# Per-token factors by a DRAM round trip instead of transposes, with a table of put-off steps, in a two-layer hybrid attention encoder

## The chip, the cores and the metric

The kernel runs on one core of a Trainium2 chip. A core has a matrix engine (TensorE, PE in the profile), VectorE (DVE), ScalarE (ACT), GpSimd (POOL) and SyncE (SP). SP computes nothing here: it issues DMAs. All engines run their own instructions in order and wait for each other by semaphores. The metric is the device time of one execution in microseconds.

## The reference, cut to what matters

512 tokens of width 1024 pass through two layers. In each layer a mixer A (8 query heads, 2 key heads, window 128, with a sink logit) and a mixer B (three head groups with other windows and dilations) run on one joint projection of x. What the change touches is how the attention outputs are scaled, token by token:

```python
# mixer A, per block:   e = exp(s - m);  denom = sum(e) + exp(sink - m)
o = einsum('nkgqs,nskd->nqkgd', e, vj) / denom
# mixer B: three group outputs, weighted per position and head slot
wts = softmax(stack(lses), axis=0)
ob = einsum('gbsh,gbshd->bshd', wts, stack(outs))
```

Then both outputs go through a branch projection, are gated (`ga * ya + gb * yb`), projected out, normalised, and followed by an MLP, a gated per-layer embedding and a second normalisation.

## The kernel before

All products are made in three passes of a float32r split: each matrix is cut into a high and a low part (`split`: ACT casts to the high part, DVE subtracts to get the low one), and hi*hi, lo*hi and hi*lo are summed (`mm3`). Weights come as tiles of 128x1024 by SP (`wst`, three buffers), are cut, and then used; some (`LATER`) are cut by `split_later`, where ACT writes -hi and an accumulating DMA issued by POOL adds the weights to it (tile `wlo`). A fetch by SP waits until the buffer's earlier weights are cut.

The attention block of a layer is one loop over small steps, `attention_block`. TensorE's order is fixed by hand while it is recorded: generators yield conditions on a forecast clock `fc`, and in each round the loop takes the first step that is due out of `side` (small helper units) and `live` (at most two attention units), and otherwise a step of the filler, which is three 128x512 matmuls of a projection (names `ps_(...)`), a gate or, at the end, the branch-A product `ya`. The other engines' order is settled by a scheduler that sees the whole program.

There are four A units (`unit_a`, names `a0` to `a3`, each two heads), six B units (`unit_b`, names `b`, pair 0 or 1, group 0 to 2) and two mixings (`mix_b`). A unit's steps on TensorE are scores (`sa`, `sb`), transposes of the probabilities (`pta`, `ptb`), and value products (`oa`, `ob`). Between them DVE masks the scores, ACT takes exponentials, ACT and DVE cut the transposed probabilities (`pth`, `ptl`). The result f (`fa`, `ogb`) has head dimensions on its 128 partitions and the 512 tokens along its rows.

The factors (`den` for A, `e` for B) come out the other way: a token is a partition. To multiply f by them, `widened` lets ACT write the factor 64 times into a 128x512 tile `wide`, four TensorE transposes turn it (tiles `rsa`, `rs`, in PSUM), and DVE multiplies (`token_scaled`). A layer does that four times for A and six times for B, 40 transposes in all. Then `split` makes the operands OA and OB of the branch products.

When the block is over, the residual tiles `y`, the embedding input `pf` and rows of constants are loaded by SP, `pf` is cut (`ph` by ACT, `pl` by DVE), and the branch products run: gates `g`, `ya` for A (which needs OA), then `yb` for B (which needs OB). A gate's projection is read out of its PSUM bank by a tanh on ACT (tile `gate`); there are three such banks (tag `mm`), taken in turn by projections, gates and `ya`.

Of the kernel before, what the change touches and what calls it, by code (L numbers as in the profile page):

```python
# [10 lines left out]
F32 = mybir.dt.float32  # L11
# [3 lines left out]
ALU = mybir.AluOpType  # L15
# [5 lines left out]
P = 128  # L21
S = 512
# [14 lines left out]
        ("b", 1, 0), ("b", 1, 1), ("b", 1, 2), ("g", 4), ("g", 5), ("y", 0), ("y", 1), ("g", 6), ("g", 7), ("y", 2), ("y", 3)]  # L37
PASSES = ((0, 0), (0, 1), (1, 0))
HOP = 0.35
ACTIVE = 2  # L40

QB0, KB0, VB0, GL0 = 768, 1536, 2304, 3072

# [158 lines left out]
def build(nc, tc, plan, down, xT, xN, pT, wst, vec, rows, sink, cst, out):  # L202
# [3 lines left out]
    with ctx:  # L206
# [142 lines left out]
        def attention_block(l, av, rp, vt, OA, OB, begun):  # L349
# [101 lines left out]
                fc.give("o", t)  # L451
                return t

            def widened(c, name, after):
                wide = av.tile([P, 4, 2, 64], F32, tag="wide", name="wide" + name, bufs=1)
                nc.scalar.copy(wide, c.rearrange("p r (j u) -> p j r u", u=1).to_broadcast([P, 4, 2, 64]))
                return wide, fc.on("act", 0.52, after) + HOP

            def token_scaled(f, wide, name, after):
                R = bank("pt", "rs" + name)  # L460
                for j in range(4):
                    nc.tensor.transpose(R[:, j * P:(j + 1) * P], wide[:, j].rearrange("p r d -> p (r d)"), ident)
                nc.vector.tensor_tensor(f, f, R, ALU.mult)
                t = fc.on("dve", 0.6, max(fc.pe(0.43) + HOP, after)) + HOP
                fc.take("pt", t)
                return t


            WIN = [(max(0, P * (j - 1)), min(S, P * (j + 2))) for j in range(4)]
# [2 lines left out]
            def unit_a(i):  # L472
# [26 lines left out]
                nc.scalar.activation(se, se, AF.Exp)  # L499
                nc.vector.tensor_tensor(den, den, se, ALU.add)  # L500
                nc.vector.reciprocal(den, den)
                wide, t_wide = widened(den, nm_, ex[1, 3] + 0.6)
                yield lambda: "va" in held
                v, t_v = held["va"]
                f = av.tile([P, S], F32, tag="f", name="f" + nm_, bufs=1)
                groups = [(r, kbs) for r in range(2) for kbs in ((0, 3), (1,), (2,))]
                done = []

# [35 lines left out]
                held["P"] -= 2  # L544
                if i == 3:
                    held["vv"] -= 1
                yield lambda: fc.open("pt") and fc.t >= t_wide
                t_f = token_scaled(f, wide, nm_, t_f)
                split(OA[i][0], OA[i][1], f)
                forecast_split(S, t_f)  # L550


            WIN0 = [(max(0, P * j - 64), min(S, P * j + 192)) for j in range(4)]
# [111 lines left out]
            def mix_b(sp, cn, cs):  # L665
# [33 lines left out]
                for g in range(3):  # L699
                    nc.vector.tensor_tensor(e[:, g], e[:, g], mn, ALU.mult)  # L700
                t += 2.6
                for g in range(3):
                    f, t_f, _ = fs[g]
                    wide, t = widened(e[:, g].rearrange("p (s b) -> p s b", s=2), f"{nm_}_{g}", t)
                    yield lambda: fc.t >= t and fc.open("pt")
                    token_scaled(f, wide, f"{nm_}_{g}", t_f)
                    t = fc.t
                f = fs[0][0]
                nc.gpsimd.tensor_tensor(f, f, fs[1][0], ALU.add)
                nc.vector.tensor_tensor(f, f, fs[2][0], ALU.add)  # L710
                split(OB[sp][0], OB[sp][1], f)

            sk = av.tile([P, 8], F32, tag="sk", name=f"sk{l}", bufs=1)
            nc.scalar.dma_start(sk, sink[l])
# [37 lines left out]
            def filler():  # L752
                def project(key, sigma_order):
                    yield lambda: held["qk"] - held["free_qk"] < 5
                    held["qk"] += 1
                    ps = yield from steps((l, key), X)
                    held[key] = rope(ps, sigma_order, "_".join(str(v) for v in (l, *key)))

                for kind, *idx in FLOW:
                    if kind == "qa":  # L760
                        yield from project(("qa", *idx), False)
                    elif kind == "b":
                        yield from project(("qb", *idx), idx[1] > 0)
                        yield from project(("kb", *idx), idx[1] > 0)
                        ps = yield from steps((l, ("vb", *idx)), X)
                        nm_ = "vb" + "_".join(str(v) for v in (l, *idx))
                        v, t = values(ps, "sigma" if idx[1] else "edge", nm_)
                        side.append([v_unit(("vb", *idx), v, t, nm_), None])
                    elif kind == "g":
                        ps = yield from steps((l, ("g", 0, *idx)), X)  # L770
                        ga.append(gate(l, 0, idx[0], vt, rp, ps))
                        fc.give("mm", fc.on("act", 0.57, fc.t + HOP) + HOP)
                    else:
                        yield lambda: not any(k[0] == "a" for k in (*waiting, *live))
                        u = idx[0]
                        w = weights((l, ("ba", u)))
                        fc.on("dve", 1.135, fc.on("act", 0.947, fc.t + HOP) + HOP)
                        for n, g in enumerate(ga[2 * u:2 * u + 2]):
                            yield lambda: fc.open("mm")
                            ps = bank("mm", f"ya{l}_{u}_{n}")  # L780
# [13 lines left out]
                    return True  # L794
                return ok

            ga, waiting, live = [], {}, {}
            for i in range(4):
                waiting["a", i] = (slots(2, "ka", ("qa", i)), lambda i=i: unit_a(i))
            for sp in range(2):  # L800
# [5 lines left out]
                waiting["m", sp] = (lambda sp=sp: not any(k[:2] == ("b", sp) for k in live),  # L806
                                    lambda sp=sp, cn=cn, cs=cs: mix_b(sp, cn, cs))
            with tc.manual_schedule(engines={PE}):
                side.append([v_unit("va", va, t_va, f"va{l}"), None])
                fill, fill_ok, idle = filler(), None, 0  # L810
                while waiting or live or side or fill:
                    if waiting and len(live) < ACTIVE:
                        key = next(iter(waiting))
                        ok, make = waiting[key]
                        if ok():
                            del waiting[key]
                            live[key] = [make(), None]
                    moved = False
                    for key, g in [(None, g) for g in side] + list(live.items()):
                        if g[1] is None or g[1]():  # L820
                            try:
                                g[1] = next(g[0])
                            except StopIteration:
                                if key is None:
                                    side.remove(g)
# [17 lines left out]

        def gate(l, b, t, vt, rp, ps=None):
            ps = linear((l, ("g", b, t)), X) if ps is None else ps
            g = rp.tile([P, S], F32, tag="gate", name=f"gate{l}_{b}_{t}", bufs=11)
            nc.scalar.activation(g, ps, AF.Tanh, bias=vt["half"][:, b * 8 + t:b * 8 + t + 1], scale=0.5)
            return g

# [209 lines left out]
        for l in range(DEPTH):  # L1059
# [31 lines left out]

            M = []
            for u in range(4):
                gs = [gate(l, 1, t, vt, rp) for t in (2 * u, 2 * u + 1)]
                w = weights((l, ("bb", u)))
                for n, g in enumerate(gs):
                    t = 2 * u + n
# [268 lines left out]
```

## Time and profile before

| | us |
|---|---|
| median of three runs | 1539.62 |
| the three runs | 1536.09, 1539.66, 1539.62 |
| the profiled execution's own time | 1536.4 |
| its span in the trace | 1534.6 |
| TensorE busy | 1512.5 (99% of the span) |
| DVE, ACT, POOL busy | 1017.7, 763.7, 246.4 |

The span runs from the first to the last instruction; 1.8 us of the time lie around it. TensorE's matmuls are pipelined and their ends are modelled, so that a busy TensorE can still hold gaps: the starts of neighbouring matmuls tell more than their durations. The two attention blocks lie at about 29 to 264 and 792 to 1032 us.

### The profile page before, as it was taken

Reading aid. Unit: us, or ns where it says so; the run is one execution under the profiler, and the core shown is the slowest. Engines: PE = TensorE matmul, PEld = TensorE weight load, DVE = VectorE, ACT = ScalarE, POOL = GpSimd, SP = SyncE. Lnnn points to the kernel's source line nnn. Section 1 sums busy time; section 2 is a strip of 40 time slices with the busy share of each in tenths; the row PEclk is TensorE's granted clock in tenths of the full one; section 3 lists DMA queues with packets and bytes.
Section 4 is the critical chain, followed back from the end, with each engine's and each line's share of the span. In section 5 each row is a group of like instructions: output and inputs, shape, how many; then the busy total and the mean of one; then the engine's idle time right before and its main releaser. Section 6 shows DMA issues by size and latency. Waiting matters only on the chain.

```text
span 1534.6 us, 19685 instructions
## 1 busy us (share of the span) xinstructions
PE 1512.5 (99%) x7438; PEld 1243.0 (81%) x7438; DVE 1017.7 (66%) x1751; ACT 763.7 (50%) x1244; POOL 246.4 (16%) x213
## 2 busy tenths in 40 slices
PE   9999999999999999999999999999999999999996
PEld 7778888888888888888887888878888888888885
DVE  5666553558568777686876665534585776767868
ACT  5777764344344443444557776633442444444442
POOL 1212220110011120202012112111100201111022
PEclk9999999999999999999999999999999999999998
DMA  7544665345612414141355445574455233231403
GB/s 234 124 112 111 149 151 166 123 137 152 205 55 87 133 54 153 42 161 59 100 168 137 114 112 138 138 209 134 149 149 183 69 109 111 82 124 56 151 1 96
DMA packets 53951, 189.47 MB, mean 123 GB/s; under 512 B 6496, under 2 KB 6880, under 8 KB 53856
## 3 DMA queue, kind: packets, MB, share of 16 engines
q1 hardware_dynamic: 43200, 151.74, 30.0%
q0 software_dynamic: 9936, 36.18, 12.5%
q8 instruction: 58, 0.95, 0.3%
q10 hardware_dynamic: 720, 0.30, 0.1%
q14 instruction: 37, 0.30, 0.1%
HBM read 155.16 MB, written 4.19 MB: 104 GB/s over the span
## 4 chain that ended last, share of the span: by engine, by line
PE 88%; DVE 5%; DMA 3%; ACT 2%; issue 1%; POOL 0%; SPq 0%; POOLq 0%; DVEq 0%; ACTq 0%
PE dn L1018 16%; PE ps_up L281 8%; PE ps_up L280 8%; PE ps_up L282 8%; PE pg L288 2%; PE wo L288 2%; PE wo L287 2%; PE wo L286 2%; PE pg L286 2%; PE pg L287 2%; PE sa L439 1%; PE pta L417 1%; DMA raw<-wst 1%; PE sb L439 1%; PE ps_start L281 1%
## 5 line engine op out<-in xcount | busy, mean ns | idle before, releaser
L228 ACT CAST whi<-wst 128x1024 fp32r<-128x1024 f32 (+2 forms) x120 | 121.2, 1010 | 257.8 <-PE ps_up L281 115.5
L229 DVE TENSOR_TENSOR wlo<-wst,whi 128x1024 fp32r<-128x1024 f32 (+2 forms) x120 | 145.5, 1216 | 128.2 <-ACT whi L228 127.4
L280 PE MATMUL ps_up<-xhi,whi 128*128 128x512 f32 x512 | 199.2, 389 | 0.0
L281 PE MATMUL ps_up<-xlo,whi 128*128 128x512 f32 x512 | 199.2, 389 | 0.0
L282 PE MATMUL ps_up<-xhi,wlo 128*128 128x512 f32 x512 | 199.2, 389 | 0.0
L991 POOL TENSOR_TENSOR hr<-r 128x512 f32<-128x512 f32 x64 | 102.2, 1597 | 552.2 <-ACT r L983 531.7
L280 PEld LDWEIGHTS ps_up<-xhi,whi 128*128 128x128 f32 x512 | 96.1, 188 | 20.0
L282 PEld LDWEIGHTS ps_up<-xhi,wlo 128*128 128x128 f32 x512 | 96.1, 188 | 19.9
L281 PEld LDWEIGHTS ps_up<-xlo,whi 128*128 128x128 f32 x512 | 96.1, 188 | 19.9
L228 ACT CAST whi<-raw 128x1024 fp32r<-128x1024 f32 x56 | 58.0, 1053 | 97.0 <-PE ps_up L281 57.7
L228 ACT CAST dhi<-raw 128x1024 fp32r<-128x1024 f32 x56 | 58.7, 1052 | 82.2 <-PE dn L1018 60.1
L1037 DVE TENSOR_TENSOR y<-y,dn 128x512 f32<-128x512 f32 x96 | 65.0, 681 | 38.7 <-PE dn L1018 38.7
L235 POOL DMA_DIRECT2D wlo<-wst x54 | 47.4, 877 | 244.8 <-ACT wlo L234 157.6
L971 DVE TENSOR_TENSOR raw<-raw,raw 128x1024 f32<-128x1024 f32 x64 | 86.3, 1348 | 0.2
L233 ACT CAST whi<-wst 128x1024 fp32r<-128x1024 f32 x54 | 56.7, 1051 | 42.5 <-PE ps_start L281 6.9
L229 DVE TENSOR_TENSOR wlo<-raw,whi 128x1024 fp32r<-128x1024 f32 x56 | 68.1, 1219 | 14.1 <-ACT whi L228 14.1
L229 DVE TENSOR_TENSOR dlo<-raw,dhi 128x1024 fp32r<-128x1024 f32 x56 | 69.2, 1238 | 5.8 <-ACT dhi L228 5.8
L234 ACT ACTIVATE wlo<-whi 128x1024 fp32r<-128x1024 f32 x54 | 57.3, 1061 | 0.9
L288 PE MATMUL pg<-bhi,xlo 128*128 128x512 f32 x128 | 49.9, 390 | 1.2 <-DVE xlo L915 1.2
L1018 PE MATMUL dn<-whi,smh 128*128 128x512 f32 x128 | 50.1, 394 | 0.7 <-DVE y L1037 0.7
L1018 PE MATMUL dn<-wlo,smh 128*128 128x512 f32 x128 | 50.6, 395 | 0.1
L1018 PE MATMUL dn<-whi,sml 128*128 128x512 f32 x128 | 49.9, 390 | 0.0
(846 smaller groups left out, 4014.0 us busy)
## 6 DMA issues: line engine op xcount, KB each, us to landing
wst<-wst SPq DMA_DIRECT2D x187, 512.0 KB, 3.5
raw<-wst SPq DMA_DIRECT2D x64, 512.0 KB, 4.2
wlo<-wst POOLq DMA_DIRECT2D x54, 512.0 KB, 4.6
y<-rows POOLq DMA_DIRECT2D x14, 512.0 KB, 7.2
row<-rows SPq DMA_DIRECT2D x7, 512.0 KB, 8.8
wst<-wst SPq DMA_DIRECT2D x9, 256.0 KB, 2.7
xs<-xT SPq DMA_DIRECT2D x8, 256.0 KB, 6.0
y<-xN SPq DMA_DIRECT2D x4, 512.0 KB, 5.7
```

What stands on the lines that cost most here:

```text
L228: nc.scalar.copy(hi, src)
L229: nc.vector.tensor_tensor(lo, src, hi.bitcast(F32), ALU.subtract)
L280: nc.tensor.matmul(ps, w[0][:, s], x[0], start=start, stop=False, skip_group_check=part)
L281: nc.tensor.matmul(ps, w[0][:, s], x[1], start=False, stop=False, skip_group_check=part)
L282: nc.tensor.matmul(ps, w[1][:, s], x[0], start=False, stop=stop, skip_group_check=part)
L286: nc.tensor.matmul(ps, x[0], w[0][:, c], start=start, stop=False)
L287: nc.tensor.matmul(ps, x[0], w[1][:, c], start=False, stop=False)
L288: nc.tensor.matmul(ps, x[1], w[0][:, c], start=False, stop=stop)
L971: nc.vector.tensor_tensor(to, to, other, ALU.add)
L991: nc.gpsimd.tensor_tensor(h.rearrange("p s t -> p (s t)"), r, r, ALU.mult)
L1018: nc.tensor.matmul(ps[s], a[:, k, tok], w[b][:, cols], start=first and not (k or m), stop=k == 3 and m == 2, skip_group_check=True)
L1037: return nc.vector.tensor_tensor(to, to, ps, ALU.subtract if n in (2, 4, 5) else ALU.add)
```

## The change

It replaces `widened` and `token_scaled`. One TensorE transpose for each A unit (128x8) and each mixing (128x24) turns the factors themselves into rows of 128 tokens (tile `rt`); ACT copies them out of PSUM and issues a DMA that writes them to a DRAM tile `line`, rows of 512 bytes; SP then issues DMAs that read four rows as one of 2 KB into 64 partitions each (tile `R`, two DMAs for each factor, ten factors a layer). The multiplication and the split after it become a helper unit of their own (`scaled_a`, `mixed_b`) that is due when the forecast clock has passed `LATENCY`, 3 us, since the transpose's copy. `ya` may start when these units are done as well. A table `LEAVE` names 26 steps of units by key and step number, and by how much forecast time each is put off after it would be due (`left`). The gates of branch B move from the pool `rp` to `np1` under a tag of their own. Buffers: f 1 to 2, `wide` (now R) 1 to 3.

```diff
+LATENCY = 3
+LEAVE = {
+    ("a", 0, 12): 2.2, ("a", 1, 2): 3.0, ("a", 1, 16): 1.5, ("a", 2, 8): 2.2, ("a", 2, 15): 3.0,
...
-            def widened(c, name, after):
-                wide = av.tile([P, 4, 2, 64], F32, tag="wide", name="wide" + name, bufs=1)
-                nc.scalar.copy(wide, c.rearrange("p r (j u) -> p j r u", u=1).to_broadcast([P, 4, 2, 64]))
-                return wide, fc.on("act", 0.52, after) + HOP
-
-            def token_scaled(f, wide, name, after):
-                R = bank("pt", "rs" + name)
-                for j in range(4):
-                    nc.tensor.transpose(R[:, j * P:(j + 1) * P], wide[:, j].rearrange("p r d -> p (r d)"), ident)
+            def in_rows(c, n, name, after):
+                tp = bank("pt", "rt" + name)
+                nc.tensor.transpose(tp[:n, :P], c, ident)
+                r = av.tile([24, P], F32, tag="rt", name="rt" + name, bufs=1)
+                nc.scalar.copy(r[:n], tp[:n, :P])
+                t = fc.on("act", 0.3, fc.pe(0.11) + HOP) + HOP
+                fc.take("pt", t)
+                line = dp.tile([24, P], F32, tag="line", name="line" + name, bufs=2)
+                nc.scalar.dma_start(line[:n], r[:n])
+                return line, max(t, after) + LATENCY
+
+            def in_columns(line, name):
+                R = av.tile([P, S], F32, tag="wide", name="R" + name, bufs=3)
+                for r in range(2):
+                    nc.sync.dma_start(R[r * 64:r * 64 + 64, :],
+                                      line[r * 4:r * 4 + 4].rearrange("j p -> (j p)").partition_broadcast(64))
+                return R
+
+            def scaled_a(i, f, R, t):
+                yield lambda: fc.t >= t
                 nc.vector.tensor_tensor(f, f, R, ALU.mult)
...
+                split(OA[i][0], OA[i][1], f)
+                forecast_split(S, fc.on("dve", 0.7, fc.t))
+                del held["oa", i]
...
-                yield lambda: fc.open("pt") and fc.t >= t_wide
-                t_f = token_scaled(f, wide, nm_, t_f)
-                split(OA[i][0], OA[i][1], f)
-                forecast_split(S, t_f)
+                yield lambda: fc.open("pt") and fc.t >= t_den
+                line, t = in_rows(den.rearrange("p r j -> p (r j)"), 8, nm_, t_f)
+                side.append([scaled_a(i, f, in_columns(line, nm_), t), None, ("oa", i), 0])
...
+                line, t = in_rows(e.rearrange("p g b -> p (g b)"), 24, nm_, t)
+                Rs = [in_columns(line[8 * g:8 * g + 8], f"{nm_}_{g}") for g in range(3)]
+                side.append([mixed_b(sp, fs, Rs, t), None, ("ob", sp), 0])
...
-                        yield lambda: not any(k[0] == "a" for k in (*waiting, *live))
+                        yield lambda: not any(k[0] in ("a", "oa") for k in (*waiting, *live, *held))
...
+            def left(g):
+                more = LEAVE.get((*g[2], g[3]), 0)
+                if not more or not g[1]():
+                    return not more and g[1]()
+                since.setdefault((*g[2], g[3]), fc.t)
+                return fc.t >= since[(*g[2], g[3])] + more
...
-            g = rp.tile([P, S], F32, tag="gate", name=f"gate{l}_{b}_{t}", bufs=11)
+            g = rp.tile([P, S], F32, tag=f"gate{b}", name=f"gate{l}_{b}_{t}", bufs=3 if b else 8)
```

The order of the instructions moves in both attention blocks alike, and nowhere else but in a few rows of DVE, ACT and SP next to them. On TensorE, at the second mixing of the second layer, there stands before (rows of `ya`, the branch-A product, and of the transposes `rs`):

```order
L462 MATMUL rs_1_0_9193<-ident,wide_1_0_9158 128x128 x4
L280 MATMUL ya_0_1_9186<-oah_6784,whi_8969 128x512
L281 MATMUL ya_0_1_9186<-oal_6785,whi_8969 128x512
L282 MATMUL ya_0_1_9186<-oah_6784,wlo_8970 128x512
L280 MATMUL ya_0_1_9186<-oah_6784,whi_8969 128x512
L281 MATMUL ya_0_1_9186<-oal_6785,whi_8969 128x512
L282 MATMUL ya_0_1_9186<-oah_6784,wlo_8970 128x512
L462 MATMUL rs_1_1_9207<-ident,wide_1_1_9199 128x128 x4
```

And in the changed kernel:

```order
L290 MATMUL ya_0_1_9182<-oah_6780,whi_9013 128x512
L291 MATMUL ya_0_1_9182<-oal_6781,whi_9013 128x512
L292 MATMUL ya_0_1_9182<-oah_6780,wlo_9014 128x512
L467 MATMUL rt_1_9195<-ident,e_1_9160 24x128
L290 MATMUL ya_1_0_9218<-oah_6780,whi_9064 128x512
```

The twelve transposes of a mixing in three groups have become a single one. On DVE, at the last A unit of the second layer (`fa_3` is its f, `sb_0_1` are scores of the B unit of pair 0, group 1, and the `ISA` rows mask them), there stands before:

```order
L229 TENSOR_TENSOR ql_qb_2_7956<-t_qb_2_7950,qh_qb_2_7955 128x512
L463 TENSOR_TENSOR fa_3_7670<-fa_3_7670,rsa_3_7983 128x512
L432 ISA pb_0_1_7992,mxb_0_1_7991<-sb_0_1_0_7993,ct_6791 128x128
L432 ISA mxb_0_1_7991 128x1
L432 ISA pb_0_1_7992,mxb_0_1_7991<-sb_0_1_0_7993,ct_6791 128x128
```

And in the changed kernel:

```order
L239 TENSOR_TENSOR vvvb_0_2_8092<-vtvb_0_2_8087,vvvb_0_2_8092 128x8x64
L485 TENSOR_TENSOR fa_3_7679<-fa_3_7679,Ra_3_8074 128x512
L442 ISA pb_0_1_8083,mxb_0_1_8082<-sb_0_1_0_8104,ct_6787 128x128
L442 ISA mxb_0_1_8082 128x1
L442 ISA pb_0_1_8083,mxb_0_1_8082<-sb_0_1_0_8104,ct_6787 128x128
```

The multiplication stands in the same place, ahead of the masks, but now waits for a DMA instead of a transpose. On ACT, where the second layer's attention block ends, there stands before (`whi` are high parts of weights, `gate_0_7` reads the last gate of branch A out of its bank):

```order
L228 CAST obh_6786<-ogb_1_0_8585 128x512
L228 CAST whi_9263<-wst_9261 128x1024
L228 CAST whi_9296<-wst_9294 128x1024
L847 ACTIVATE gate_0_6_9292<-ps_('g', 0, 6)_9267,vhalf_6779 128x512
L228 CAST ph_9808<-pf_9810 128x1024
L228 CAST whi_9329<-wst_9327 128x1024
L847 ACTIVATE gate_0_7_9325<-ps_('g', 0, 7)_9300,vhalf_6779 128x512
L228 CAST whi_9363<-wst_9361 128x1024
```

And in the changed kernel:

```order
L238 CAST whi_9288<-wst_9286 128x1024
L880 ACTIVATE gate_0_6_9284<-ps_('g', 0, 6)_9259,vhalf_6775 128x512
L238 CAST obh_6782<-ogb_1_0_8666 128x512
L238 CAST whi_9321<-wst_9319 128x1024
L880 ACTIVATE gate_0_7_9317<-ps_('g', 0, 7)_9292,vhalf_6775 128x512
L238 CAST whi_9355<-wst_9353 128x1024
L238 CAST ph_9800<-pf_9802 128x1024
L238 CAST whi_9409<-wst_9407 128x512
```

The cut of `pf` has moved behind the gate and one more cast. On SP the loads of `y` and `pf` have moved behind three fetches of weights that stood among them.

## Rows read from the trace of the kernel before

**Rows 1.** The page's busy times: busy us, share of the span, instructions

```profile
PE 1512.5 (99%) x7438; PEld 1243.0 (81%) x7438; DVE 1017.7 (66%) x1751; ACT 763.7 (50%) x1244; POOL 246.4 (16%) x213
```

**Rows 2.** Busy time of each engine by stretch (us from the start): both attention blocks, last branch

```profile
29.20:240.10 210.90, 210.66 (x1272) 171.54 (x1271) 130.81 (x374) 149.90 (x325) 43.16 (x49) 1.00 0.52 126
792.10:1003.40 211.30, 211.07 (x1275) 171.88 (x1274) 131.20 (x377) 150.14 (x326) 43.24 (x49) 1.00 0.52 126
1026.60:1063.00 36.40, 34.45 (x153) 28.18 (x152) 15.02 (x16) 11.05 (x14) 4.72 (x4) 1.00 0.63 207
```

**Rows 3.** What TensorE waited for, whole span: us, times, longest

```profile
PE ya L280 <- ACT gate L847: 1.9, 1, 1.9
...
PE rs L462 <- ACT wide L456: 0.4, 2, 0.2
```

**Rows 4.** Timeline of TensorE at one group of four transposes: start, duration

```profile
246.46 0.40 PE L282 MATMUL ya<-oah,wlo 128*128 128x512 f32 x1
246.69 0.60 PE L462 MATMUL rs<-ident,wide 128*128 128x128 f32 x4
247.05 0.48 PE L280 MATMUL ya<-oah,whi 128*128 128x512 f32 x1
247.37 0.39 PE L281 MATMUL ya<-oal,whi 128*128 128x512 f32 x1
```

**Rows 5.** Timeline of TensorE where passes of 128 columns follow each other

```profile
235.87 0.22 PE L652 MATMUL ob<-pthb,vvvb 128*64 128x128 f32 x1
...
235.93 0.22 PE L652 MATMUL ob<-ptlb,vvvb 128*64 128x128 f32 x1
```

**Rows 6.** Timeline of ACT where the second layer's attention block ends

```profile
1031.81 1.05 ACT L228 CAST ph<-pf 128x1024 fp32r<-128x1024 f32 x1 [8.75 <-DMA pf<-pT]
1032.76 1.04 ACT L228 CAST whi<-wst 128x1024 fp32r<-128x1024 f32 x1
1033.71 0.68 ACT L847 ACTIVATE gate<-ps_('g', 0, 7)_9300,vhalf 128x512 f32<-128x512 f32 x1
```

**Rows 7.** Timeline of TensorE at the same place

```profile
1032.10 0.39 PE L282 MATMUL ya<-oah,wlo 128*128 128x512 f32 x1
1034.44 0.50 PE L280 MATMUL ya<-oah,whi 128*128 128x512 f32 x1 [1.95 <-ACT gate L847]
```

**Rows 8.** Timeline of SP's DMA issues at the same place

```profile
1022.09 0.97 SPq L1081 DMA_DIRECT2D y<-kept  x2
1023.11 0.47 SPq L1112 DMA_DIRECT2D pf<-pT  x1
```

**Rows 9.** DMA issues: count, KB each, median us to landing; the last: tile row alone

```profile
wst<-wst SPq DMA_DIRECT2D x9, 256.0 KB, 2.7
...
kept<-y SPq DMA_DIRECT2D x4, 512.0 KB, 2.8
...
sk<-sink ACTq DMA_DIRECT2D x2, 4.0 KB, 4.1
...
DMA to landing us min/median/max: 3.7/8.8/13.6
```

**Rows 10.** What SP's queue waited for at 29 to 300 us

```profile
SPq L249 <- DMA wlo<-wst: 214.4, 26, 13.5
```

**Rows 11.** Work at 29.2 to 240 us by form: busy us, mean ns

```profile
L432 DVE CUSTOM_DVE_ANT_0 pb<-sb,ct 128x128 f32<-128x128 f32 x32 | 7.1, 286 | 3.5 <-PE sb L439 3.5
L432 DVE DVE_READ_ACCUMULATOR2_ANT mxb<- 128x1 f32 x48 | 4.0, 83 | 0.0
L463 DVE TENSOR_TENSOR fa<-fa,rsa 128x512 f32<-128x512 f32 x4 | 2.7, 680 | 0.0
...
L234 ACT ACTIVATE wlo<-whi 128x1024 fp32r<-128x1024 f32 x23 | 24.4, 1062 | 0.4
...
L428 ACT ACTIVATE pb<-pb,cs 128x128 f32<-128x128 f32 x32 | 12.4, 388 | 4.5 <-DVE cs L603 4.5
L456 ACT COPY widea<-dena 128x512 f32<-128x512 f32 x4 | 2.5, 616 | 0.1
```

More of the change, by code (lines that the diff above doesn't have):

```diff
@@ L39 @@
 HOP = 0.35
+LATENCY = 3
 ACTIVE = 2
+LEAVE = {
[6 rows of a table added]
+}
 QB0, KB0, VB0, GL0 = 768, 1536, 2304, 3072
@@ L452, in join @@
                 return t
-            def widened(c, name, after):
-                wide = av.tile([P, 4, 2, 64], F32, tag="wide", name="wide" + name, bufs=1)
-                nc.scalar.copy(wide, c.rearrange("p r (j u) -> p j r u", u=1).to_broadcast([P, 4, 2, 64]))
-                return wide, fc.on("act", 0.52, after) + HOP
-            def token_scaled(f, wide, name, after):
-                R = bank("pt", "rs" + name)
-                for j in range(4):
-                    nc.tensor.transpose(R[:, j * P:(j + 1) * P], wide[:, j].rearrange("p r d -> p (r d)"), ident)
-                nc.vector.tensor_tensor(f, f, R, ALU.mult)
-                t = fc.on("dve", 0.6, max(fc.pe(0.43) + HOP, after)) + HOP
-                fc.take("pt", t)
-                return t
+            def in_rows(c, n, name, after):
[8 more added lines that the diff above has]
+                return line, max(t, after) + LATENCY
@@ L469, in attention_block, with mixed_b @@
+            def mixed_b(sp, fs, Rs, t):
+                yield lambda: fc.t >= t
+                for (f, _, _), R in zip(fs, Rs):
+                    nc.vector.tensor_tensor(f, f, R, ALU.mult)
+                f = fs[0][0]
+                nc.gpsimd.tensor_tensor(f, f, fs[1][0], ALU.add)
+                nc.vector.tensor_tensor(f, f, fs[2][0], ALU.add)
+                split(OB[sp][0], OB[sp][1], f)
             WIN = [(max(0, P * (j - 1)), min(S, P * (j + 2))) for j in range(4)]
@@ L501, in unit_a @@
                 nc.vector.reciprocal(den, den)
-                wide, t_wide = widened(den, nm_, ex[1, 3] + 0.6)
+                t_den = ex[1, 3] + 0.6
+                held["oa", i] = True
                 yield lambda: "va" in held
                 v, t_v = held["va"]
-                f = av.tile([P, S], F32, tag="f", name="f" + nm_, bufs=1)
+                f = av.tile([P, S], F32, tag="f", name="f" + nm_, bufs=2)
                 groups = [(r, kbs) for r in range(2) for kbs in ((0, 3), (1,), (2,))]
@@ L701, in mix_b @@
                 t += 2.6
[L702 to L711, printed above, removed]
+                yield lambda: fc.t >= t and fc.open("pt")
+                line, t = in_rows(e.rearrange("p g b -> p (g b)"), 24, nm_, t)
+                Rs = [in_columns(line[8 * g:8 * g + 8], f"{nm_}_{g}") for g in range(3)]
+                side.append([mixed_b(sp, fs, Rs, t), None, ("ob", sp), 0])
             sk = av.tile([P, 8], F32, tag="sk", name=f"sk{l}", bufs=1)
@@ L767, in filler @@
                         v, t = values(ps, "sigma" if idx[1] else "edge", nm_)
-                        side.append([v_unit(("vb", *idx), v, t, nm_), None])
+                        side.append([v_unit(("vb", *idx), v, t, nm_), None, ("vb", *idx), 0])
                     elif kind == "g":
@@ L795, in slots @@
                 return ok
-            ga, waiting, live = [], {}, {}
+            def left(g):
[4 more added lines that the diff above has]
+                return fc.t >= since[(*g[2], g[3])] + more
+            ga, waiting, live, since = [], {}, {}, {}
             for i in range(4):
@@ L808, in attention_block @@
             with tc.manual_schedule(engines={PE}):
-                side.append([v_unit("va", va, t_va, f"va{l}"), None])
+                side.append([v_unit("va", va, t_va, f"va{l}"), None, ("va",), 0])
                 fill, fill_ok, idle = filler(), None, 0
@@ L816, in attention_block @@
                             del waiting[key]
-                            live[key] = [make(), None]
+                            live[key] = [make(), None, key, 0]
                     moved = False
                     for key, g in [(None, g) for g in side] + list(live.items()):
-                        if g[1] is None or g[1]():
+                        if g[1] is None or left(g):
                             try:
                                 g[1] = next(g[0])
+                                g[3] += 1
                             except StopIteration:
@@ L1093, in build @@
             for u in range(4):
-                gs = [gate(l, 1, t, vt, rp) for t in (2 * u, 2 * u + 1)]
+                gs = [gate(l, 1, t, vt, np1) for t in (2 * u, 2 * u + 1)]
                 w = weights((l, ("bb", u)))
```

5 rows, old and new, of the table LEAVE are left out of this document.

## The prediction

> **What bounds the kernel now.** I read the busy times first: TensorE is busy 99% of the span [rows 1], every other engine at most two thirds. Its share could hide gaps, so I read both attention blocks by stretch next: 210.9 and 211.3 us, with less than 0.3 us in each in which TensorE does nothing, at full granted clock [rows 2]. The third stretch is where the second layer's block ends: 34.45 of 36.40 us busy, so 1.95 us are missing there, and only in that layer. The list of waits puts names to it: one wait of 1.9 us for a gate, and 0.4 us in two waits for `wide` [rows 3]. So the block is a chain of TensorE work with almost no waits. An edit pays here if it takes passes from TensorE, or removes that one gap; it costs if it makes TensorE wait.
>
> **What it removes from TensorE.** Four transposes cost it 0.36 us (246.69 to 247.05), and the first matmul behind them stands 0.32 us ahead of its successor where 0.23 is usual [rows 4]. Passes of 128 columns follow each other at 0.06 us [rows 5]. So the group is four passes, 0.24, and a change of kind costs about 0.1 on each side. That gives two prices: 0.06 for a 128-column pass and 0.1 for each change of kind. In the program's order I counted, from the first transposes of v to the third `ya` unit, 185 runs of one kind before and 170 after in each layer (the filler alone goes from 63 runs to 55), and 34 transposes fewer (40 less 6). That is 34 x 0.06 + 15 x 0.1 = 3.5 us a layer, 7.1 in both. The table's part is in the 15 runs; with waits of 0.4 us in both blocks together there are no others that it could remove.
>
> A pass of 128 columns takes 0.22 us from start to end, but its neighbour starts 0.06 later [rows 5]; I price by starts. The Trainium skill ("TensorE: Matmul & The Clock Gate", Part 4: PE-mode transpose) gives about 275 ns for a transpose in a kernel's context. By it 68 transposes would be worth 18.7 us instead of 4.1, and the sum below would be 22.2. The rows show that this is a duration and no pitch.
>
> ACT is rid of ten copies of 616 ns a layer [rows 11], and DVE multiplies as often as before. Both are off the path, and I cost that at nothing.
>
> **The gap in the second layer.** TensorE stops between 1032.10 and 1034.44, which is 2.34 where 0.23 is usual: 2.1 us [rows 7]. It waits for a gate's bank. ACT reads that bank out at 1033.71, because the cut of `pf` stands two places ahead of it on ACT and had waited 8.75 us for its DMA [rows 6], issued just behind two loads of `y` [rows 8]. After the change the gate stands ahead of the cut, as the order shows. SP issues three fetches ahead of the four `y` and `pf`, so `pf` lands later still, but behind it on ACT now come casts that TensorE wants a branch unit later. I take the whole 2.1 us.
>
> **What it adds: a trip through DRAM.** In-order engines make it a matter of who is queued behind. On DVE the multiplication by R has masks or cuts behind it, which TensorE wants. On SP the fetches of weights stand behind the reads of R; SP sits 214.4 of 271 us waiting for the accumulating DMAs anyway [rows 10], and fetched data waits for a free buffer afterwards, so a few us there are covered. If that cover were gone, a fetch would come late by as much as R waits for `line`.
>
> The trace has no such trip, so I bound it. Transposing, hop and copy: 0.6, as a whole wide copy takes 616 ns [rows 11]. The write of 4 KB: 2.7 to 4.1 to landing, as the shortest rows show 2.7 for a fetch and 2.8 for a write, and a 4 KB load 4.1 [rows 9]. The read: 0.5 for the first of two issues [rows 8] and 2.7 to 3.7, where 3.7 is the fastest broadcast; in the crowd that is 8.8 [rows 9]. Together 6.5 to 8.9, and 14.0 with the crowd's 8.8. I take 6.9, near the low end: the blocks' DMA share is 0.52 [rows 2], and the crowded rows belong to stretches of `y` and constants.
>
> The Trainium skill ("DMA: Bandwidth & Descriptors", Anatomy of one DMA) gives 2.0 us plus bytes over 436 GB/s for each DMA, and warns that the receipt of a write to HBM can take surprisingly long. By its figure the trip would be an estimated 5.4 us and no place below would stall, which adds 1.6 us to the gain. Its warning is the slower rival, with the trip set by rows.
>
> How long may the trip be? For A unit 3 TensorE has 11.4 us of work between `rt` and `ptb_0_1_0`, by the order: 33 wide passes at 0.23, 44 narrow ones mostly at 0.06, ten changes of kind. After R come the multiplication 0.68, four masks of 0.37, four exponentials of 0.39 and hops, 3.9 together [rows 11]. That leaves 7.5, and since a `wlo` of 1.06 stands ahead of the write on ACT, 6.4. The same working gives 6.6 for the first mixing (12.7 of work; eight masks, two multiplications and four exponentials are 6.1), 7.8 for A unit 0 (11.0; five DVE operations, 3.2), 9.3 for A unit 1. A unit 2 and the last mixing have much more. At 6.9 the two tightest places stall by 0.5 and 0.3: 0.8 a layer, 1.6 in both. A trip of 6.4 gives 0, one of 8.9 gives 5.9 a layer.
>
> **The sum.** 7.1 + 2.1 - 1.6 = 7.6 us off the profiled execution: 1536.4 to 1528.8, span 1527.0. Two of the three runs shown lie at 1539.6 and one at 1536.09, near the profiled one. Half-way, 1538.0, I put the base: 1530.4 us.
>
> **Rivals.**
> - The trip eats the gain. Stalls a layer are three times the trip less 20.8 (the three limits), and the 9.2 us gained are used up at a trip of 8.5; the time is over 0.3% slower from 9.5. At 10, with a read of 5.3 between the quiet 3.7 and the crowded 8.8, that is 9.9 a layer (A unit 1 joins in), 19.8 in all, 1548.6. For it: in the crowd both `row` and the 4 KB load are slow [rows 9]. Against: half the DMA time is free in the blocks.
> - The trip lies between 8 and 9.5: 1535 to 1544, no difference that can be told.
> - The gap of 2.1 us stays in another form. The cut `pl` on DVE stands ahead of the multiplications that free the banks of the last `ya`; should `pf` land some 20 us after its issue, TensorE waits there instead. Then 1532.5.
> - Transposes cost TensorE their duration, not their pitch: then the saving is 14.6 larger, 1515.8. Rows 5 speak against it, as said.
>
> **How the numbers follow.** The forecast and the third rival, both faster: 0.53 and 0.17. The trip between: 0.18. The trip at 9.5 or more: 0.10. The last rival: 0.02. Measurements of this kernel tell about 0.3%, 4.6 us: faster means under 1535.0, slower over 1544.2. So 0.72, 0.18 and 0.10. The likeliest case alone spans 1526.9 (no stall, from the fastest run) to 1535. The range is 1525 to 1542: the bound of no stalls below, and above a trip of 9.2.
>
> **What would show it right or wrong.** Right: both stretches from the transposes of v to the third `ya` unit shorter by about 3 us each; no wait of `ya` for a gate near 1025 us; the write landing in about 2.7 and the read in 3.2. Wrong: DVE idle before the multiplication by R with a DMA as releaser and TensorE's waits naming `pth`, `ptl` or masks right after; SP waiting for `line` so long that ACT's casts wait for `wst`; or a new wait of TensorE in the branch for `pl`'s followers.

## The result

The changed kernel takes 1542.24 us (13 runs, 1539.53 to 1544.56) against 1539.62 (13 runs, 1535.03 to 1540.99): ratio 1.0022, 95% interval 1.0013 to 1.0031. It is 0.2% slower, by the prediction's bound of 0.3% no difference, where 7.6 us less than the profiled execution were forecast; 1542.24 lies just above the range. The profiled execution took 1541.4 (span 1539.6), near its median; that of before took 1536.4, 3 us under its own.

The page's busy times of the changed kernel (busy us, share of the span, instructions), to stand beside [rows 1]:

```profile
PE 1508.2 (98%) x7370; PEld 1236.7 (80%) x7370; DVE 1015.2 (66%) x1751; ACT 754.5 (49%) x1236; POOL 247.0 (16%) x213
```

The 68 transposes are gone (7438 to 7370) and TensorE is busy 4.3 us less, but the span is 5 us longer. Busy time by stretch of the changed kernel, as in [rows 2]: both attention blocks up to the first `ya`; then three pieces of the first block, and one of the second layer's branches (the columns behind POOL are granted clock, DMA share, GB/s):

```profile
29.35:244.80 215.45, 210.34 (x1247) 169.74 (x1246) 129.03 (x371) 146.74 (x324) 43.09 (x49) 0.99 0.55 132
795.05:1008.40 213.35, 208.34 (x1246) 168.44 (x1245) 128.82 (x371) 146.69 (x324) 43.01 (x49) 1.00 0.55 134
204.00:205.60 1.60, 0.67 (x5) 0.68 (x5) 0.00 (x0) 1.60 (x3) 0.00 (x0) 0.85 0.32 115
205.60:208.80 3.20, 3.20 (x10) 2.58 (x9) 2.50 (x18) 1.18 (x3) 0.86 (x1) 0.54 0.81 170
208.80:212.00 3.20, 3.20 (x15) 2.63 (x15) 3.17 (x7) 2.32 (x11) 1.29 (x1) 1.00 0.92 230
1052.60:1062.60 10.00, 7.67 (x34) 5.78 (x33) 6.22 (x6) 4.62 (x7) 2.99 (x2) 1.00 0.66 195
```

Where TensorE missed 0.24 us in a block, it now misses 5 in each. After one of these gaps it runs at the lower of its two clocks (1.2 GHz) for about 3 us: 10 instructions in 3.2 us at 0.54, where the next 3.2 us hold 15. The list of waits says who was waited for (us, times, longest):

```profile
ACT oah L238 <- DVE fa L485: 29.3, 8, 6.8
DVE fa L485 <- DMA Ra<-linea: 28.7, 8, 5.4
...
DVE ogb L493 <- DMA R<-line: 14.5, 4, 4.8
...
PE vtvb L417 <- ACT vTvb L403: 3.8, 4, 1.4
...
PE ob L683 <- DVE ogb L459: 2.6, 4, 0.8
...
PE yb L290 <- ACT gate L880: 2.3, 1, 2.3
...
PE oa L454 <- DVE ptla L239: 1.6, 2, 0.8
...
PE ptb L427 <- DVE cs L634: 1.3, 2, 0.7
```

All twelve first multiplications by R stop DVE, 43.2 us together, and ACT stops at the cut behind those of the A units. One such place, A unit 0 of the first layer, in the timeline (start, duration, what ended the idle time before):

```profile
70.81 0.27 PE L467 MATMUL rta<-ident,dena 128*8 128x128 f32 x1
70.92 0.60 PE L427 MATMUL pta<-ident,pa 128*128 128x128 f32 x4
...
71.96 0.26 ACT L469 COPY rta<-rta 8x128 f32<-8x128 f32 x1
...
72.25 0.53 ACTq L473 DMA_DIRECT2D linea<-rta  x1
...
76.12 1.14 SPq L479 DMA_DIRECT2D Ra<-linea  x2
...
80.72 0.69 DVE L485 TENSOR_TENSOR fa<-fa,Ra 128x512 f32<-128x512 f32 x1 [3.31 <-DMA Ra<-linea]
...
81.44 0.62 ACT L238 CAST oah<-fa 128x512 fp32r<-128x512 f32 x1 [3.44 <-DVE fa L485]
...
82.49 0.45 PE L453 MATMUL oa<-ptha,vvva 128*128 128x384 f32 x1 [0.50 <-ACT ptha L238]
...
83.79 0.39 PE L454 MATMUL oa<-ptla,vvva 128*64 128x384 f32 x1 [0.85 <-DVE ptla L239]
```

From transpose to multiplication the trip takes 9.9 us here. Behind it ACT and DVE reach the cuts `ptha` and `ptla` late, and TensorE waits for both. Over the twelve trips (to a mixing's first multiplication): 7.4 to 9.9, mean 8.6, of which 1.3 to the write's issue, 2.4 to the read's and 4.9 to the multiplication. And at the second layer's end [rows 6, 7] there is again a gap, one branch later:

```profile
1043.46 1.05 ACT L238 CAST ph<-pf 128x1024 fp32r<-128x1024 f32 x1 [6.03 <-DMA pf<-pT]
1044.41 0.62 ACT L238 CAST whi<-wst 128x512 fp32r<-128x512 f32 x1
...
1054.85 1.04 ACT L238 CAST whi<-wst 128x1024 fp32r<-128x1024 f32 x1 [9.82 <-DMA wst<-wst]
1055.80 0.68 ACT L880 ACTIVATE gate<-ps_('g', 1, 0)_9413,vhalf 128x512 f32<-128x512 f32 x1
...
1056.53 0.50 PE L290 MATMUL yb<-obh,whi 128*128 128x512 f32 x1 [2.33 <-ACT gate L880]
```

### The profile page after: what moved, and what is told of

Same layout as the page of the kernel before. It is cut to its first block, busy times and chain, and to the rows that moved or that the text cites. A ratio compares the mean times of both kernels' runs of the same rounds, so it can differ in the third digit from the quotient of the medians.

```text
span 1539.6 us, 19634 instructions
## 1 busy us (share of the span) xinstructions
PE 1508.2 (98%) x7370; PEld 1236.7 (80%) x7370; DVE 1015.2 (66%) x1751; ACT 754.5 (49%) x1236; POOL 247.0 (16%) x213
## 4 chain that ended last, share of the span: by engine, by line
PE 82%; DMA 6%; DVE 6%; ACT 3%; issue 2%; SPq 0%; POOL 0%; ACTq 0%; DVEq 0%; POOLq 0%
PE dn L1051 15%; PE ps_up L291 8%; PE ps_up L292 8%; PE ps_up L290 8%; DMA wst<-wst 2%; PE pg L298 2%; PE wo L298 2%; PE wo L297 2%; PE wo L296 2%; PE pg L297 2%; PE pg L296 2%; DMA Ra<-linea 2%; PE sa L449 1%; DMA wlo<-wst 1%; DMA raw<-wst 1%
```

## The experiments

**Three theories.** T: the trip is longer than forecast, DVE and ACT stand in it, and TensorE's operands stand behind. W: the new order of steps makes waits of its own, wherever R comes from. For the end of the second block: P, `ph` stands too early on ACT; Q, the loads there (four `y`, `pf`, two rows, 3.5 MB) hold up fetches of weights.

Each run was timed beside the kernel before on the same chip; ratios are to that one, whose medians lay between 1539.43 and 1540.29. "Block" is the time from the first transposes of v to the first gate of branch B in the profiled execution, first and second layer. Where the text says that TensorE's order is kept, it is the same row for row. A profiled execution need not lie at the median: that of the changed kernel with late loads took 1542.10, the slowest of its 12 runs.

| kernel | us (median) | ratio, interval | block 1, 2 |
|---|---|---|---|
| before | 1539.62 | | 245.7, 247.8 |
| changed | 1542.24 | 1.0022 [1.0013, 1.0031] | 248.8, 246.8 |
| before, late cut | 1533.42 | 0.9964 [0.9951, 0.9976] | 245.5, 245.7 |
| before, late loads | 1533.27 | 0.9960 [0.9948, 0.9972] | 245.5, 245.5 |
| changed, late loads | 1537.65 | 0.9993 [0.9983, 1.0003] | 251.5, 247.8 |
| no trip, late loads | 1531.86 | 0.9951 [0.9937, 0.9965] | 244.7, 244.7 |
| changed, late loads, entry | 1540.52 | 1.0010 [0.9999, 1.0021] | 248.0, 247.8 |
| no trip, late loads, entry | 1524.36 | 0.9907 [0.9891, 0.9924] | 241.1, 241.0 |
| the same with trip, put off 4 | 1532.06 | 0.9958 [0.9941, 0.9975] | 243.9, 244.8 |
| put off 4, mixings 9 | 1529.89 | 0.9934 [0.9921, 0.9948] | 243.9, 244.0 |

**No trip.** R from the input:

```diff
-  line[r * 4:r * 4 + 4].rearrange("j p -> (j p)").partition_broadcast(64))
+  xN[0][r, 0:S].partition_broadcast(64))
```

> The changed kernel, but R is read from the input x (rows of the same 2 KB, to the same 64 partitions), so that no read waits for the factors; the write of `line` stays and nothing reads it. The output is not the reference's: the factors are replaced. TensorE's order is that of the changed kernel, instruction for instruction. Theory T (the trip through DRAM is 7.4 to 9.9 us where 6.9 was forecast, and DVE and ACT stand in it with TensorE's next operands behind): the gaps of TensorE behind the multiplications go, by the trace of the changed kernel about 7 us in the first layer (1.8, 0.5, 1.6, 1.7 and 1.4 at half clock) and 5 in the second: 1530, from 1528 to 1533. Rival W (the new order, by the table and the put-off multiplications, makes the waits, whatever R comes from): within 3 us of the changed kernel, 1539 to 1543. The gap of 2.3 us at the end of the second layer's block is neither's and may go or stay.

Measured 1542.62, ratio 1.0017 [1.0008, 1.0026]: by the time alone T fell. The waits tell more:

```profile
PE ya L290 <- ACT gate L880: 7.3, 1, 7.3
PE vtvb L417 <- ACT vTvb L403: 3.0, 2, 1.5
```

In the first block the waits for `oa`, `ptb` and half of those for `ob` are gone, and it is 4.3 us shorter (248.8 to 244.5). But the gap at the second block's end has grown to 7.3 us, and `vtvb` waits 1.5 us a layer without any trip: that part is W's. The end had to be kept alike before anything else could be priced.

**Three other edits of the order.** LATENCY 3 to 6; the table emptied; an A unit's factors transposed and sent ahead of its transposes and value products:

```diff
                 held["oa", i] = True
+                yield lambda: fc.open("pt") and fc.t >= t_den
+                line, t_R = in_rows(den.rearrange("p r j -> p (r j)"), 8, nm_, 0)
+                R = in_columns(line, nm_)
```

> The changed kernel with LATENCY 6 instead of 3: the multiplications by R come 3 us of forecast time later, when by the trips measured R has nearly landed. Theory T: DVE and ACT wait for R about 3 us less in each of twelve places (43 us in all before), TensorE's gaps there shrink to a third or less: 1533 to 1537. Rival W: the new order moves the waits to other places: 1540 or more.

> The changed kernel with an empty table of put-off steps; all else as it is. Theory T: the trips stay and stall TensorE as much, and the filler is cut into some more runs: 1541 to 1547. Rival W (the table put steps where they wait for banks, as the new waits for `ob` of 1.0 and 0.7 us a layer): those go, 1537 to 1540.

> The changed kernel, but an A unit's factors are transposed, written and read as soon as they are ready, ahead of its value products, and only the multiplication stays behind them. The trip then runs beside the unit's own 10 us and more of transposes and value products. Theory T: the four waits of DVE for `Ra` a layer (28.7 us in all) go, and with them TensorE's gaps behind them (1.8, 0.5 and 1.6 us in the first layer, 0.9, 0.9 and 1.6 in the second); those of the mixings stay: 1533 to 1537. Rival W: no change of more than 2 us, 1540 to 1544, since the order makes the waits.

LATENCY 6: 1570.52, 1.0198 [1.0178, 1.0218], a miss. DVE still waited 39.8 us for R: LATENCY moves steps in TensorE's order, while DVE's place for the multiplication hardly changes; with waits for R nearly as long as before, the kernel is 28 us slower, and TensorE's longest waits are now 8.0 us at `sb` and 5.4 at `vtvb`. Empty table: 1545.77, 1.0040 [1.0028, 1.0053], as T has it; the table is worth some 3 us to the changed kernel. Early factors: 1543.61, 1.0022 [1.0012, 1.0032]. No multiplication waits for `Ra` any more, yet TensorE now waits 2.8 us at `sa`, and at `oa` 3.3 us instead of 2.1, as W has it; this run's step numbers were off by one behind the new step. With the numbers moved along and late loads it was slower still:

> The changed kernel with late loads and with the A units' factors sent ahead of their transposes and value products, the table's step numbers moved with them. The trips of A units are then hidden as in the earlier run of that kind; its new waits (for `oa`, `sa`) came partly from a table whose numbers were off by one. Theory T: 3 to 5 us under the changed kernel with late loads: 1532 to 1536. Rival W (a table made for another order cuts as much as the trips): within 2 us of it.

1554.57, 1.0099 [1.0086, 1.0113], with waits of 2.1 us and more for `oa` and `sb`. Both forecasts missed: this new order brought waits larger than what it saved.

**The end of the block.** First the cut alone is held behind the fourth gate of branch B; nothing else moves:

```diff
-            split(ph, pl, pf)
+            with tc.issue_after(gate_ins[l, 1, 3]):
+                split(ph, pl, pf)
```

> The changed kernel, with the cut of `pf` held behind the fourth gate of branch B on ACT (`ph`; its `pl` on DVE follows); nothing else moves. Theory P (at the end of the second layer's block ACT's cast `ph` waits for `pf`, the next cast, its cut on DVE and so a fetch of weights come late, and TensorE waits 2.5 us for a gate behind that cast): the gap and 0.3 us at half clock go, 1539.4, from 1538 to 1541. Rival Q (the fetch is late because four `y`, `pf` and two rows land in the same stretch, whoever cuts them): no change, 1541 to 1543.

> Both at once: R from the input, so no trip, and the cut of `pf` held behind the fourth gate. The output is not the reference's (the factors are replaced). Theory T with P: without the trip the blocks are 4 us a layer shorter than in the changed kernel, and what hid that in the run without the trip was the gap of 7.4 us with 11 matmuls at half clock at the second block's end; with the cut out of the way it is gone: 1533, from 1531 to 1536. Rival W (the order alone): 1539 or more.

> The kernel before, with only the cut of `pf` held behind the fourth gate of branch B. Theory P: its gap of 2.1 us goes, ratio 0.9986 to before, some 1537.9. Rival Q: no change, 0.9995 to 1.0005.

Changed kernel: 1541.38, 1.0014 [1.0004, 1.0025], no gain; no trip: 1543.15, 1.0026 [1.0014, 1.0038], a wait of 6.6 us for a gate left. Kernel before: 1533.42. So P holds for the kernel before and Q for the changed one, where ACT's cast waits for the fetch itself (timeline of the changed kernel with late cut):

```profile
1056.60 1.04 ACT L238 CAST whi<-wst 128x1024 fp32r<-128x1024 f32 x1 [12.02 <-DMA wst<-wst]
```

In the kernel before, holding back the cut is worth 6.1 us at the median, three times the gap that its profile showed. Its runs, which lay between 1535.67 and 1542.34 us (20 runs), then lie between 1532.80 and 1534.43 (5 runs). Then the loads themselves were moved behind fetches that TensorE needs sooner, on SP, and the additions to `y` behind sums of gates, on POOL:

```diff
-            for a in range(4):
-                nc.sync.dma_start(y[a], kept[a] if l else xN[a])
...
+                for a in ((), (0, 1), (2, 3), ())[u]:
+                    with tc.issue_after(last_fetch[0]):
+                        nc.sync.dma_start(y[a], kept[a] if l else xN[a])
...
-            nc.sync.dma_start(pf, pT[l])
+            with tc.issue_after(last_fetch[0]):
+                nc.sync.dma_start(pf, pT[l])
```

> The changed kernel, with the loads of the next stage moved behind fetches of weights: two `y` each behind the fetches traced at the second and third pair of branch-B gates, `pf` and the two rows behind those at the last, and the additions to `y` on POOL behind the sums of the gates. TensorE's order is unchanged. Theory Q (at the second block's end 3.5 MB of loads stand ahead of fetches that TensorE needs): the wait for a gate there goes, 2.5 us and its half clock in the profiled run, more where the crowd was worse: 1536 to 1540. Rival P (the cut of `pf` alone): no better than with the late cut, 1541.

> R from the input, so no trip, with the same late loads (output not the reference's: the factors are replaced). Theory T with Q: the wait of 6.6 us for a gate, the two of 1.4 for `wlo` and the half clock behind them go: 1530 to 1533, which is 5 to 9 us under the changed kernel with late loads, the price of the trip. Rival W: within 2 us of that kernel.

> The kernel before with the same late loads: what the end of its second block costs without the crowd. Theory Q: as with the late cut alone, 1532 to 1535. With it the change itself, both ends alike, is priced: by theory T the changed kernel with late loads is 3 to 6 us slower than this one, and without the trip 1 to 3 us faster.

1537.65, 1531.86 and 1533.27, and none of the three waits for a gate at that place: Q. (In the kernel before, late loads are worth as much as the late cut, 1533.27 and 1533.42.) With both ends alike, the change is 4.4 us slower than the kernel before; the trip's price is 5.8 (1537.65 to 1531.86); without the trip it is 1.4 faster. The shorter transposing shows up as far less than the 3.5 us a layer forecast.

**Where the rest is.** Without the trip one long wait is left in each block, at `vtvb` (timeline of the kernel without trip, with late loads):

```profile
197.04 0.51 ACT L439 ACTIVATE pb<-pb,cn 128x256 f32<-128x256 f32 x1 [2.42 <-DVE cn L617]
...
198.91 1.03 ACT L243 CAST whi<-wst 128x1024 fp32r<-128x1024 f32 x1
199.85 0.58 ACT L404 COPY vTvb<-ps_('vb', 1, 1)_2104 128x512 f32<-128x512 f32 x1
...
200.48 0.79 PE L418 MATMUL vtvb<-ident,vTvb 128*128 128x128 f32 x4 [1.49 <-ACT vTvb L404]
```

The copy that TensorE wants stands on ACT behind four exponentials, which wait for masks, and a cast. Behind the wait the granted clock is 0.55 for 2.8 us (10 instructions):

```profile
200.60:203.40 2.80, 2.80 (x10) 2.32 (x11) 1.37 (x3) 2.80 (x10) 0.86 (x1) 0.55 0.35 117
```

One more entry puts that step off:

```diff
-    ("vb", 1, 0, 1): 0.3,
+    ("vb", 1, 0, 1): 0.3, ("vb", 1, 1, 1): 2.2,
```

> The changed kernel with late loads and one more entry in the table: the transposes `vtvb` of pair 1, group 1 are put off by 2.2 us of forecast time. Theory V (part of the gain is lost to one new wait a layer of 1.6 us, TensorE at `vtvb` for a copy of v that stands on ACT behind four exponentials, and to about 1.4 us at half clock behind it): up to 3 us a layer come back, 1532 to 1536. Rival: the steps that move with the entry cut new waits of the same size, and the time stays within 2 us of the changed kernel with late loads.

> The same entry in the kernel without the trip and with late loads (output not the reference's: the factors are replaced). Theory V: no gap over 1 us is left in the blocks, and the kernel is 5 to 6 us faster than without the entry, 1526 to 1528: then the whole of the saving of TensorE passes read from the traces, 9 to 10 us, is seen against the kernel before with late loads. Rival: within 2 us of the kernel without the entry.

Without the trip: 1524.36, 7.5 us less than without the entry and 8.9 less than the kernel before with late loads. Its blocks hold no gap over 0.3 us (the first layer's: 241.05 long, TensorE busy 240.95):

```profile
29.44:270.49 241.05, 240.95 (x1395) 195.77 (x1394) 144.62 (x400) 157.48 (x338) 46.61 (x52) 1.00 0.55 135
```

So W has its part, and the whole saving is there once waits are gone. With the trip the entry doesn't help: 1540.52, 2.9 above the kernel without the entry, a miss for V's forecast. With the entry the trip costs 16.2 us (1524.36 to 1540.52), since the steps that moved stand behind multiplications that wait (its list of waits):

```profile
DVE fa L486 <- DMA Ra<-linea: 28.1, 8, 5.4
...
DVE ogb L494 <- DMA R<-line: 17.7, 6, 3.9
...
PE ob L454 <- ACT pthb L238: 2.9, 2, 1.4
```

**Length or place?** The trip stays, TensorE's order too; only the multiplication and its cuts are put off, and held on DVE behind the last mask recorded by then:

```diff
+                put_off.append((fc.t + LATER_BY, put))
...
+                    with tc.issue_after(last_mask[0]):
+                        put_off.pop(0)[1]()
```

> The changed kernel with late loads and the further table entry, computing all of the reference; TensorE's order is that of the two runs before, instruction for instruction. Only the multiplications by R and the cuts behind them are put off by 4 us of forecast time and held behind the masks that stand ahead of them then, so that DVE and ACT reach them when R has landed. Theory T (the trip costs only because DVE and ACT stand in it with TensorE's operands behind): most of the 16 us between the runs with and without the trip come back: 1525 to 1530. Rival: the multiplications crowd DVE where they stand now, and it stays above 1535.

> The same with 6 us. Theory T: as with 4 us, or 1 to 2 us better where a trip took over 9 us: 1524 to 1529. Rival: above 1535.

By 4 us: 1532.06, 8.5 under the same kernel without it, where T wanted 1525 to 1530. DVE waits for `Ra` 3.5 us in place of 28.1, and the waits of TensorE behind the A units, at `oa` and `vtvb`, are gone. What is left are waits for `pthb` and `ptlb` at the first mixings (list of waits, put off by 4):

```profile
DVE ogb L502 <- DMA R<-line: 14.1, 9, 3.4
...
DVE fa L491 <- DMA Ra<-linea: 3.5, 3, 1.2
...
PE ob L456 <- ACT pthb L239: 2.6, 2, 1.4
...
PE ob L457 <- DVE ptlb L240: 2.2, 2, 1.1
```

By 6: 1534.02, 0.9964 [0.9950, 0.9978], no better; the exponentials of an A unit's scores come late instead (`pta` waits 2.0 us). The mixings' multiplications were then put off further, behind the last cut as well:

> As the run put off by 4 us, computing all of the reference, TensorE's order the same; only the mixings' multiplications are put off by 9 us of forecast time and held behind the last cut that DVE was given, where the run before it left 3 us a layer of waits (TensorE at `ob` for `pthb` and `ptlb`) behind the first mixing's three multiplications. Theory T: those 2.9 us of waits a layer go, 1524 to 1528. Rival: they move to the operands that now stand behind the multiplications, 1530 to 1534.

1529.89, 0.9934 [0.9921, 0.9948], 9.7 us under the kernel before and faster than both kernels of this study. Of the 9.7, 6 are those of the late loads: against the kernel before with late loads (1533.27) the change gains 3.4. `ogb` no longer waits for R; as the rival has it, the waits have moved, to one of 1.4 us a layer at `sb` with some 3 us at a lower granted clock behind it (0.63 in the first layer, 0.73 in the second; its list of waits):

```profile
DVE fa L493 <- DMA Ra<-linea: 3.1, 3, 1.4
...
PE sb L454 <- DVE ql_kb L242: 2.8, 2, 1.4
```

**A read that was meant to be shorter.** One DMA to 128 partitions instead of two to 64 each:

```diff
-                for r in range(2):
-                    nc.sync.dma_start(R[r * 64:r * 64 + 64, :],
...
+                nc.sync.dma_start(R, line[0:8].rearrange("(r j) p -> r (j p)", r=2).unsqueeze(1).to_broadcast([2, 64, S]))
```

> The changed kernel, but each factor's R is read by one DMA to all 128 partitions instead of two to 64 each; the second of two issues ended 1.1 to 1.9 us after the first began. Theory T (TensorE's stalls follow the trip's length): the trip is about 1 us shorter, and at three waits a layer that is 4 to 6 us: 1536 to 1539. Rival W: within 1.5 us of the changed kernel.

1649.57, 1.0723 [1.0704, 1.0742]. The trip became longer: the read issued at 75.57 let DVE go at 86.89, 11.3 us where the two had needed 4.6:

```profile
86.89 0.69 DVE L483 TENSOR_TENSOR fa<-fa,Ra 128x512 f32<-128x512 f32 x1 [9.68 <-DMA Ra<-linea]
```

As a test of T it works the other way round: trips of 13.8 us in the mean to the first multiplication, instead of 8.6, cost 107, with DVE waiting 138.3 us for R instead of 43.2. The packets of the trace show where the time goes in this first trip. Both ways 128 packets of 2 KB move. In the two DMAs up to 19 are in flight at once, and all start between 78.27 and 79.85 us. In the one DMA, whose pattern is 2 by 64 where theirs is 64, never more than three are in flight, and they start between 78.38 and 86.47. Whether it is the pattern that does this no run shows, since none varied it alone.

## Why the prediction was wrong

With late loads as the common ground the difference splits into four steps (us, medians). They add up to 2.8, where 2.6 were measured, and each is uncertain by 1 to 2:

| step | forecast | measured | from |
|---|---|---|---|
| fewer TensorE passes | -7.1 | -8.9 | before to no trip, with entry |
| waits of the new order | 0 | +7.5 | with entry to without, no trip |
| the trip | +1.6 | +5.8 | no trip to trip, without entry |
| end of the second block | -2.1 | -1.6 | its gap 6.2 before, 4.6 after |

How rows two and three share their sum depends on which is taken out first: with the entry the trip costs 16.2, and beside the trip the order's wait costs nothing (with the entry 2.9 more). Their sum doesn't depend on it: 13.3 us of waits. That is the step that failed: the sum took 1.6 us of stalls for the trip and nothing for waits of the new order. The prediction's own first sign of being wrong came: DVE idle before the multiplications by R with a DMA as releaser, and TensorE waiting for `ptha` and `ptla` right after.

**Passes: right, and undersized.** Blocks go from 245.5 to 241.05, 4.5 a layer in place of 3.5; busy time alone by 4.1. With 34 passes at 0.06, 2.0, the fewer runs of one kind are worth 2.1. In this order, with the entry, they are 12 fewer and not 15 (188 to 176 in a block of the trace; 173 in the changed kernel), so 0.17 each in place of 0.1. The rival that transposes cost their duration falls: it wanted 18.7. The new transpose lasts 0.27, as the Trainium skill has it ("TensorE: Matmul & The Clock Gate", Part 4: PE-mode transpose). The next matmul starts 0.11 behind it (70.81 to 70.92), so that is no pitch.

**Waits of the new order: put at nothing.** "The table's part is in the 15 runs ... there are no others that it could remove" asked what waits the table could take away, not what waits a new order brings. The copy `vTvb` behind four exponentials was to be seen in ACT's order, but not how late the masks would be. Without the trip, the run with one more entry shows the price: 7.5 us, half clock included.

**The trip: mechanism right, size wrong.** 6.9 was taken, 8.6 measured. It lies inside the bounds of 6.5 to 8.9; the choice near the low end was wrong. The first part was 1.3 rather than 0.6 (ACT gets to the copy late), the second 2.4 rather than 2.7 or more, the third 4.9 where 3.2 to 4.2 was allowed: the fastest broadcast was no fair price. At 8.6 the formula gives 3 x 8.6 - 20.8 = 5.0 a layer; the runs without the entry say 2.9, and in the changed kernel's profiled execution the waits of TensorE that the kernel without the trip does not have (`oa`, `ptb`, the longer ones at `ob`, the shorter ones at `vtvb`) add up to some 3 a layer. The tight places named were A unit 3 and the first mixing. A unit 3 stalled, the first mixing only with the entry; A units 0 and 2 stalled as well, since a blocked ACT holds back `ptha` (unit 0) and `vTvb` (unit 2, 0.3 and 0.7 us), which the limits, counted on DVE, left out. The estimate of 5.4 from the Trainium skill ("DMA: Bandwidth & Descriptors", Anatomy of one DMA) is 3.2 under the mean; that section gives its formula for DMAs issued by GpSimd, and here ACT and SP issue them. Its warning on receipts of writes does not explain the difference, since the write's part, 2.4, is no longer than was allowed, and the read was issued as little as 1.25 us after the write.

**The gap at the end: moved.** "I take the whole 2.1 us" fails: `pf` does land later, and the casts a branch later are those that TensorE then wants. That they would wait for a fetch behind 3.5 MB of loads, rather than for `pl`, no rival had. At the median 1.6 of 6.2 us went.

**The rival that fits.** By number the second rival came in: the trip between 8 and 9.5, no difference that can be told. That is in part luck. By its formula a trip of 8.6 stalls 10.0 us and gives 1538.8; in the runs without the entry the trip cost 5.8, and waits of the new order, which no rival had, more than made up for it.

**The base** was 1538.0; 1539.6 is the kernel before's median over its 13 runs, so 1.6 us of the miss lie there.

What stays open: why in the kernel before this gap is 2.1 us in the profiled execution and costs 6.1 at the median; no profile caught a slower one.

## What to carry to other kernels

A trip through DRAM is paid not by its length alone but by what stands behind its consumer on in-order engines: the same trip cost 16 us, or under 6, by the place of ten multiplications a layer. A later forecast time for the step did not set that place (LATENCY 6); one together with an ordering edge on DVE did. Where TensorE has no slack, ask of any new order which waits it adds, engine by engine, and try the order with the suspected wait taken out (constant data, the same instructions). And look at the end of a stage before pricing its middle: a burst of loads there can eat a gain, or hide it.

## What the runs showed of the hardware

After a wait of 1.35 us at `vtvb` (by starts, TensorE was 1.6 us late) in the first layer of the changed kernel, TensorE ran at half clock for some 3 us (granted 0.54, then 1.00), which nearly doubles the price of the gap. After the same wait in the second layer it did not (granted 1.00), nor after the 1.95 us in the kernel before [rows 7]. And one broadcasting read to 128 partitions, with a pattern of 2 by 64, took 11.3 us to its consumer, against 4.6 for two to 64 partitions each: at most three of its 2 KB packets were in flight at once, against up to 19.
